# First sum of h in the head, scans issued with their scores, and shifted filler rates in a two-layer decoder trunk

## The chip, the core and the metric

One NeuronCore of a Trainium2 chip runs the whole program. TensorE (PE) multiplies matrices, VectorE (DVE), ScalarE (ACT) and GpSimd (POOL) do elementwise work, SyncE (SP) issues the DMAs. The metric is the device time of one execution in microseconds (us); the time of the kernel before is the median of three runs.

## The reference

Two layers, each on a residual stream x of 1024 tokens by 1024 features, all in float32:

```python
h = rmsnorm(x, norm1[l])
proj = h @ w_in[l]
qa, ka, va, qb, kb, vb, gate_pre = jnp.split(proj, splits, axis=-1)
o_a = dilated_mixture(hd4(qa), hd4(ka), hd4(va))          # 3 groups x 4 heads, softmax with ALiBi
o_b = stick_breaking_attention(hd4(qb), hd4(kb), hd4(vb)) # 4 heads
gates = jax.nn.sigmoid(gate_pre + b_gate[l])
merged = g_a * (o_a @ w_br[l, :OUT_A]) + g_b * (o_b @ w_br[l, OUT_A:])
x = x + merged @ w_o[l]
# then: rmsnorm, up-projection, causal depthwise conv, gelu * value, down-projection, residual
```

In stick-breaking attention a query's weight on a key is sigmoid(z) times the product of (1 - sigmoid(z)) over all later keys up to the query: a product that runs backwards along the row of keys.

## The kernel before

**Arithmetic.** Every float32 factor is kept as two parts, hi (rounded to the matmul's type) and lo (the rest): `split` makes them, hi with a cast on ACT (L141) and lo with a subtraction on DVE (L146). A product is three matmuls of 128 x 512: hi·hi, hi·lo, lo·hi. Larger products (`pair`, `up`, `down`) are done on 2 x 2 blocks with seven block products instead of eight; for these the blocks of h, called b11, b12, b21 and b22 in the code, have to be added and subtracted first, into S[1], S[2], S[3] and S[4], each four tiles of 128 x 512 in two parts. `block_sums` does that: S[3] begins from b22 and b12, S[1] from b12 and b11, each with three POOL operations per tile (L988, L993, L994); S[2] comes from S[1] and b22, S[4] from S[2] and b21, with two DVE operations per tile (L1004, L1005); each is then split in two.

**The mixer of a layer.** Its first part is the head: values, keys and queries of the first two stick heads by plain products (`values_part`, `kq_half`), while the last parts of h are still being made. Then `attend` goes through a list of items: 16 stick items (`stick_item`, four heads by four blocks of 256 queries, the longest block first), four near items (`near_item`, window attention with dilation 1) and 16 far items (`far_item`, the two dilated groups). An item has steps: scores into the PSUM banks "s" (L619, L620); exponentials or sigmoids on ACT; turns (transposes of the weights by PE, then a split in two); applies (products with the values). `attend` issues the next item's scores between the steps of the current one.

In a stick item, a row's scores get the causal mask on DVE (L683), two sigmoids on ACT (L684 into beta, L685 into stay), and then the backward product, a scan on DVE (L697), and a product of beta with it (L701). The scans wait in a list, SCANS; `turn` takes from it what its own transposes need and then two more.

**The filler.** All other projections of the layer are done between these steps, so that PE has work while the other engines make the weights: four gates as plain products (`gate`, 8 shares each), ten pairs of keys, queries and values, and six pairs of gates (`pair`, 14 shares each). A share is six matmuls of 128 x 512. `Dense.advance(rate)` is called once after each step of an item and adds the rate to what is due; whole shares are issued. The rates are RATE for stick items (by the block's length, RATE[3] for the longest), RATE_N for near and RATE_T for far ones. Where a fetch is not there, `until` issues shares until it is declared done, a fixed number of shares after its issue: LEAD for stick rows and far items, LEAD_N for near items. What filler is left behind the last item, `finish` issues, and then come the rest of the two joins of the branches, the split of the branch inputs and the branch products (`br_ps`).

`advance` and `until` also call `aside`, which takes one entry from the list that `block_sums` returned, if the names it needs are done ("plain": the four plain gates).

**What sets the order.** PE's order is the program's, as issued. DVE, ACT and POOL are ordered by the compiler's planner by priorities and its own costs (in the feed-forward part their order is fixed too); some orders are tied by hand with add_manual_dep. All engines then take their work strictly in that order. DMAs go through SP's queue.

**Buffers.** Tiles come from rotating sets by tag: "xa" has four (stick rows' keys and values, their queries, the stay tiles, later the far items' keys and queries), "ql" two (the value tiles of the head, then each pair's weights `in_a`), "e8" six (among them S[1] to S[3], later the parts of the branch inputs), "pt" six small ones. The temporary of the sums, h_sum, is one xa tile that is held from the first sum to the end of S[4].

Of the kernel before, what the change touches and what calls it, by code (L numbers as in the profile page):

```python
# [7 lines left out]
F32 = mybir.dt.float32  # L8
# [4 lines left out]
ALU = mybir.AluOpType  # L13
# [3 lines left out]
P = 128  # L17
# [3 lines left out]
HF = 512  # L21
# [6 lines left out]
SCALE = 0.125  # L28
# [12 lines left out]
IN_ORDER = {ET.PE, ET.Activation, ET.DVE, ET.Pool}  # L41
HEAD = 4
SECOND = 0.35
RATE = (1.0, 1.15, 1.25, 1.3)
RATE_N = 0.85
RATE_T = 0.75
PLAIN = 4
LEAD = 6
LEAD_N = 9
AHEAD_B = 3  # L50
X_AT = (3, 5, 7, 9)
AHEAD = 200
# [3 lines left out]
def f32(ap):  # L56
    return ap.bitcast(F32)
# [3 lines left out]
def trunk_kernel(ctx, tc, x, norm1, w_in, b_gate, w_br, w_o, norm2, w_up, conv_w, conv_b, w_down, norm_f, out, depth=None, probe=None):  # L61
# [156 lines left out]
    class Dense:  # L218
# [38 lines left out]
        def fetch(self):  # L257


            def there(i):  # L260
                return i < 16 and {"N11", f"1{i // 8}", f"2{i // 8}", "v1", "v2"} <= self.done

            def row(j):
                return j < 16 and f"K{j // 4}" in self.done and self.rows >= j - 3

            def row_v(j):
                return j < self.b and self.free[3 - j % 4] >= j // 4

            def whole(v):
                return v < 4 and self.b == 16 and self.rows == 16 and {f"K{4 + v}", f"V{4 + v}"} <= self.done and self.near >= v  # L270

            while row(self.b):
                fetch_row(self.b)
                self.at(LEAD, lambda j=self.b: self.done.add(f"FB{j}"))
                self.b += 1
            while row_v(self.bv):
                fetch_values(self.bv)
                self.bv += 1
            while whole(self.n):
                fetch_whole(self.n)  # L280
                self.at(LEAD_N, lambda v=self.n: self.done.add(f"FN{v}"))
                self.n += 1
            while self.kq < self.scored + 2 and there(self.kq):
                fetch_kq(self.kq)
                self.at(LEAD, lambda i=self.kq: self.done.add(f"F{i}"))
                self.kq += 1
            while self.v < self.applied + 4 and there(self.v):
                fetch_v(self.v)
                self.v += 1
# [217 lines left out]
    def norm(n, gain, tag, then=None, keep=False):  # L507
        acc = ACC[n]
        ss = sb.tile([P, 8], F32, tag="ss", bufs=2, name="ss")
        yield  # L510
        tot = bank(tag, "nrm_t")
        for c in range(4):
            pe.matmul(tot[:, c : c + 1], acc[:, c * P : (c + 1) * P], ones, start=True, stop=True, skip_group_check=True)
        yield
        act.activation(ss[:, 0:4], tot[:, 0:4], AF.Sqrt, bias=eps[:, 0:1], scale=1.0 / D)
        dve.reciprocal(ss[:, 4:8], ss[:, 0:4])
        if then:
            table(then, ss[:, 4:5])
        yield
        rb = bank(tag, "nrm_b")  # L520
        for c in range(4):
            pe.transpose(rb[:, c * P : (c + 1) * P], ss[:, 4 + c : 5 + c].to_broadcast([P, P]), ident)
        yield
        new_h(n)
        for e in range(KD):
            hf = kept_f32(n, e) if keep else small("hf")
            dve.scalar_tensor_tensor(hf, xc(n, e), gain[:, e : e + 1], rb, ALU.mult, ALU.mult)
            hi, lo = H[n][0][:, e, :], H[n][1][:, e, :]
            act.copy(hi, hf)
            (pool if e % 2 and not (keep and n) else dve).tensor_tensor(lo, hf, f32(hi), ALU.subtract)  # L530
            if e < KD - 1:
                yield

# [42 lines left out]
    def in_parts(c, scale, hi, lo, x):  # L576
        if c:
            act.mul(hi, x, scale)
            return dve.scalar_tensor_tensor(lo, x, scale, f32(hi), ALU.mult, ALU.subtract)
        act.copy(hi, x)  # L580
        return dve.tensor_tensor(lo, x, f32(hi), ALU.subtract)

    def kq_half(c, w, n):
        o = bank("ps", "kq_ps"[c:])
        yield from product(o, [(w[k], h_part(n, k)) for k in range(KD)])
        hi, lo = small("kq_h", F32R), small("kq_l", F32R)
        LAST["head"] = in_parts(c, SCALE, hi, lo, o).ins.name
        keep_kq(c, n, 0, hi, lo)
        yield

# [74 lines left out]
    def stick_item(dense, u, qp):  # L665
# [4 lines left out]
        def score(a):  # L670
            L = P * (2 * qp + a + 1)
            bt = rows[a] = sb.tile([P, T], F32, tag="p4", bufs=4, name="beta")
            if a == 0:
                st[0] = sb.tile([P, 2, T], F32, tag="xa", bufs=4, name="stay")
            sv = st[0][:, a, :]
            for c1 in range(L, 0, -512):
                c0 = max(0, c1 - 512)
                w = c1 - c0
                z = bank("s", "z")
                scores(z[:, :w], *(q[:, x, a * P : a * P + P] for x in range(2)), k[:, c0:c1])  # L680
                with tc.high_priority(offset=AHEAD):
                    if c1 == L:
                        dve.tensor_tensor(z[:, w - P : w], z[:, w - P : w], mask_b, ALU.add)  # L683
                    act.activation(bt[:, c0:c1], z[:, :w], AF.Sigmoid)  # L684
                    act.activation(sv[:, c0:c1], z[:, :w], AF.Sigmoid, scale=-1.0)  # L685
                (SCANS if c1 == L else left).append((shared, bt, sv, c0, c1, L))
            if a:
                SCANS.extend(left)
                dense.rows += 1

        def scans(most):

# [284 lines left out]
    def block_sums(more):  # L977


        keep = {}  # L980

        def first(t, a, b, i):
            if i == 0:
                if "r" not in keep:
                    keep["r"] = quarter("h_sum")
                new_s(t)
            r, (ah, al), (bh, bl) = keep["r"][:, i, :], a()[i], b()[i]
            one = pool.tensor_tensor(r, f32(al), f32(bl), ALU.subtract)  # L988
            if "last" in keep:
                tc.add_manual_dep(one.ins, keep["last"], NO_SYNC, reason="one sum after the other")  # L990
            else:
                tc.add_manual_dep(one.ins, LAST["head"], SYNC, reason="after the first projections")
            pool.tensor_tensor(r, r, f32(ah), ALU.add)  # L993
            keep["last"] = pool.tensor_tensor(r, r, f32(bh), ALU.subtract).ins.name  # L994

        def further(t, a, i):
            if t == 4:

                S[4] = half(0, 0)
            less(a, i)  # L1000

        def less(a, i):
            r, (ah, al) = keep["r"][:, i, :], a()[i]
            dve.tensor_tensor(r, f32(ah), r, ALU.subtract)  # L1004
            dve.tensor_tensor(r, r, f32(al), ALU.add)  # L1005

        def in_two(t, i):
            split(*S[t][i], keep["r"][:, i, :], "waits")

        b11, b12, b21, b22 = (lambda n=n, k=k: half(n, k) for k in range(2) for n in (1, 0))  # L1010
        todo = []

        def series(after, t, f, lag, gap):

            at = {}
            for i in range(4):
                at.setdefault(i * gap, []).append(lambda i=i: f(i))
                at.setdefault(i * gap + lag, []).append(lambda i=i: in_two(t, i))
            for k in range(3 * gap + lag + 1):
                todo.append((after, lambda fs=at.get(k, ()): [g() for g in fs]))  # L1020

        series(set(), 3, lambda i: first(3, b22, b12, i), 3, 2)
        series(set(), 1, lambda i: first(1, b12, b11, i), 3, 2)
        for i in range(4):
            todo.append((set(), lambda i=i: less(b22, i)))
        series(set(), 2, lambda i: i or new_s(2), 0, 1)
        todo += more
        series({"plain"}, 4, lambda i: further(4, b21, i), 1, 1)
        return todo

    def zeros():
# [179 lines left out]
    def mixer(l, pending):  # L1211
# [7 lines left out]
        if l:  # L1219
# [3 lines left out]
                for _ in range(HEAD if i == 0 else i % 3 > 0):  # L1223
                    next(units, None)
            for _ in units:
                pass
        else:
            first_units = relay(head(l))

# [10 lines left out]
                if i == 1:  # L1240
                    next(vectors)
            for _ in first_units:
                pass
        for _ in vectors:
            pass
        dense.main = [
# [624 lines left out]
    def first():  # L1871
# [64 lines left out]
        def normed(i):  # L1936

            n, c = i // 4, i % 4
            if c == 0:
                new_h(n)  # L1940
            rb = bank("o", "x_rb")
            pe.transpose(rb[:, 0:P], factor[i][:, 2:3].to_broadcast([P, P]), ident)
            for h in range(2):
                hf = small("hf").rearrange("p (e t) -> p e t", e=4)
                for k in range(4 * h, 4 * h + 4):
                    dve.scalar_tensor_tensor(hf[:, k - 4 * h, :], part[i][:, k, :], g0[:, k : k + 1], rb[:, 0:P], ALU.mult, ALU.mult)
                split(*(y[:, 4 * h : 4 * h + 4, c * P : (c + 1) * P] for y in H[n]), hf)

        def in_two(i, *halves):
            n, c = i // 4, i % 4  # L1950
# [116 lines left out]
```

## Time and profile before

| | |
|---|---|
| median of 3 runs | 2725.03 us (2724.64 to 2726.55) |
| the profiled execution | 2720.71 us, of which the span is 2718.9 us |
| granted TensorE clock, mean | 0.992 |
| PE busy | 2648.2 us |
| DVE busy | 2079.8 us |
| ACT busy | 1341.5 us |
| POOL busy | 680.1 us |

Times in the profile are microseconds from the start of the span. A row of instructions gives start, duration, engine, line of the kernel, operation, output and inputs; in brackets stands how long the engine had been idle before it and what released it. A row of a wait gives who waited for whom, the total, the number of times and the longest. A row of a group gives busy time, mean ns of one, and the idle time before. Matmuls are pipelined: in an undisturbed stretch the starts tell their rate, not the durations.

### The profile page before, as it was taken

The page shows a single profiled execution, that of the slowest core. Times are in us where ns is not written, and L with a number is a line of the kernel's source. Part 1 is how long each engine was busy: PE and PEld are TensorE (multiplying, and loading weights), DVE is VectorE, ACT ScalarE, POOL GpSimd, SP SyncE. Part 2 cuts the span into 40 slices and gives each one's busy share as a digit, 9 for nine tenths or more (in the row PEclk, how much of TensorE's full clock was granted, in tenths as well). Part 3 has the DMA queues.
Part 4 walks back from the last instruction along what each step waited for, and adds up shares of the span by engine and source line. Part 5 has one row for each costly group of instructions (what it writes and reads, how often), then busy time and mean ns, then how long its engine had stood idle before and what let it go on. Part 6 is the DMA issues. An engine that isn't in the chain of part 4 may idle for free. (4 is left out here: it accounts for less than half of the span.)

```text
span 2718.9 us, 36768 instructions
## 1 busy us (share of the span) xinstructions
PE 2648.2 (97%) x12780; PEld 2204.5 (81%) x12780; DVE 2079.8 (76%) x3151; ACT 1341.5 (49%) x2488; POOL 680.1 (25%) x483
## 2 busy tenths in 40 slices
PE   9899999989999999999999999999899999999999
PEld 8677788878888888888887778888788888888888
DVE  5787766676789888897649777656858888998865
ACT  5455555555455545432335555654745545554225
POOL 2601011013124433421152011010312433443210
PEclk9999999989999999999999999999899999999999
DMA  8456576564334444588452657755732444546863
GB/s 276 117 136 168 150 205 194 191 229 151 93 117 158 145 155 140 212 326 312 177 159 78 162 154 191 207 171 181 268 97 82 148 150 145 171 140 250 330 250 122
DMA packets 418918, 482.95 MB, mean 178 GB/s; under 512 B 26420, under 2 KB 336044, under 8 KB 416940
## 3 DMA queue, kind: packets, MB, share of 16 engines
q1 hardware_dynamic: 418716, 480.59, 55.1%
q8 instruction: 101, 1.65, 0.3%
q14 instruction: 85, 0.70, 0.1%
q10 hardware_dynamic: 16, 0.00, 0.0%
HBM read 307.43 MB, written 173.08 MB: 177 GB/s over the span
## 5 line engine op out<-in xcount | busy, mean ns | idle before, releaser
L146 DVE TENSOR_TENSOR w_lo<-up_a,w_hi 128x512 fp32r<-128x512 f32 x240 | 237.8, 997 | 20.6 <-ACT w_hi L141 20.6
L141 ACT CAST w_hi<-up_a 128x512 fp32r<-128x512 f32 x240 | 149.4, 622 | 184.3 <-PE u_a L972 45.1
L1062 POOL TENSOR_TENSOR u<-in_a 128x512 f32<-128x512 f32 x32 | 44.1, 1380 | 702.1 <-DMA in_a<-in_w_in_dram 165.8
L1703 DVE TENSOR_TENSOR x<-x,d_ps 128x512 f32<-128x512 f32 (+1 forms) x228 | 151.8, 671 | 77.9 <-PE d_ps L1697 76.5
L1434 POOL TENSOR_TENSOR cv<-cv 128x512 f32<-128x512 f32 x88 | 132.3, 1516 | 250.0 <-DVE cv L1429 133.5
L141 ACT CAST w_hi<-in_a 128x512 fp32r<-128x512 f32 x192 | 119.5, 623 | 129.7 <-PE i_c L972 39.7
L146 DVE TENSOR_TENSOR w_lo<-in_a,w_hi 128x512 fp32r<-128x512 f32 x192 | 138.3, 722 | 56.6 <-ACT w_hi L141 52.3
L146 DVE TENSOR_TENSOR g<-cv,g 128x512 fp32r<-128x512 f32 x154 | 152.0, 988 | 5.2 <-ACT g L141 2.7
L1695 PE MATMUL d_ps<-gd_in,w_hi 128*128 128x512 f32 (+1 forms) x340 | 130.4, 384 | 1.6 <-issue 0.8
L1697 PE MATMUL d_ps<-gd_in,w_lo 128*128 128x512 f32 (+1 forms) x340 | 129.8, 382 | 0.0
L1696 PE MATMUL d_ps<-gd_in,w_hi 128*128 128x512 f32 (+1 forms) x340 | 129.8, 382 | 0.0
L971 PE MATMUL u_a<-hh,w_hi 128*128 128x512 f32 x320 | 124.7, 390 | 0.8 <-DVE u L1585 0.8
L973 PE MATMUL u_a<-hh,w_lo 128*128 128x512 f32 x320 | 124.5, 389 | 0.0
L972 PE MATMUL u_a<-t_lo,w_hi 128*128 128x512 f32 x320 | 124.5, 389 | 0.0
L971 PE MATMUL u_a<-t_hi,w_hi 128*128 128x512 f32 x320 | 124.5, 389 | 0.0
L972 PE MATMUL u_a<-hl,w_hi 128*128 128x512 f32 x320 | 124.5, 389 | 0.0
L973 PE MATMUL u_a<-t_hi,w_lo 128*128 128x512 f32 x320 | 124.5, 389 | 0.0
L146 DVE TENSOR_TENSOR w_lo<-w_raw,w_hi 128x512 fp32r<-128x512 f32 x96 | 75.6, 791 | 56.4 <-ACT w_hi L141 55.3
L141 ACT CAST g<-cv 128x512 fp32r<-128x512 f32 x154 | 94.9, 616 | 40.4 <-POOL cv L1434 29.8
L1695 PE MATMUL d_ps<-gd_in,wd 128*128 128x512 f32 (+1 forms) x292 | 113.9, 390 | 0.0
L1697 PE MATMUL d_ps<-gd_in,wd 128*128 128x512 f32 (+1 forms) x292 | 112.8, 386 | 0.0
L1696 PE MATMUL d_ps<-gd_in,wd 128*128 128x512 f32 (+1 forms) x292 | 112.8, 386 | 0.0
(394 smaller groups left out, 8556.0 us busy)
## 6 DMA issues: line engine op xcount, KB each, us to landing
gd<-g SPq DMA_DIRECT2D x154, 512.0 KB, 3.5
gd_in<-gd SPq DMA_DIRECT2D x154, 512.0 KB, 6.1
up_a<-in_w_up_dram SPq DMA_DIRECT2D x80, 512.0 KB, 5.7
in_a<-in_w_in_dram SPq DMA_DIRECT2D x64, 512.0 KB, 5.2
t_kq<-tk SPq DMA_DIRECT2D x32, 768.0 KB, 4.5
wd_raw<-in_w_down_dram SPq DMA_DIRECT2D x22, 1024.0 KB, 12.0
gin<-gs SPq DMA_DIRECT2D x32, 512.0 KB, 4.3
w_raw<-in_w_o_dram SPq DMA_DIRECT2D x64, 256.0 KB, 2.9
```

Source lines behind the costliest of these rows:

```text
L141: one = act.copy(hi, src)
L146: two = dve.tensor_tensor(lo, src, f32(hi), ALU.subtract)
L971: pe.matmul(o, w[0][:, c], rh, start=(first and i == 0), stop=False, skip_group_check=True)
L972: pe.matmul(o, w[0][:, c], rl, start=False, stop=False, skip_group_check=True)
L973: pe.matmul(o, w[1][:, c], rh, start=False, stop=(last and i == 3), skip_group_check=True)
L1062: pool.tensor_tensor(u2, a11, a21, ALU.subtract)
L1434: return lambda: pool.tensor_tensor(dst, a, b, ALU.subtract)
L1695: pe.matmul(o[:, sub], wh[:, c], gh[:, sub], start=(i == 0 and k in (0, 4, 5)), stop=False, skip_group_check=True)
L1696: pe.matmul(o[:, sub], wh[:, c], gl[:, sub], start=False, stop=False, skip_group_check=True)
L1697: pe.matmul(o[:, sub], wl[:, c], gh[:, sub], start=False, stop=(i == m - 1), skip_group_check=True)
L1703: dve.tensor_tensor(x, x, o[:, sub], ALU.add)
```

## The change

- S[3] is begun in the head: the entries of the sums are also taken there, one per step of the head that is left when all of h is made; the first POOL operation waits for the last part of h (LAST["h"]) instead of for the first projections (LAST["head"]). S[1] and what follows need the new name "head", which is set when the head has been issued.
- The temporaries: S[3] has an xa tile of its own, given back when S[3] is made; S[1] and S[2] share a tile of the tag ql; S[4] is made from S[2]'s two parts with three DVE operations per tile in small tiles.
- A stick item issues two entries of SCANS right behind its second row of scores.
- The rates: stick items 1.0, 1.15, 1.25, 1.3 become 1.15, 1.3, 1.4, 1.45; near items 0.85 becomes 0.75; far items 0.75 becomes 0.5. LEAD_N goes from 9 to 7, and far items' fetches are declared done after LEAD_T = 3 shares instead of 6.

```diff
-RATE = (1.0, 1.15, 1.25, 1.3)
-RATE_N = 0.85
-RATE_T = 0.75
+RATE = (1.15, 1.3, 1.4, 1.45)
+RATE_N = 0.75
+RATE_T = 0.5
...
-LEAD_N = 9
+LEAD_N = 7
+LEAD_T = 3
...
-                self.at(LEAD, lambda i=self.kq: self.done.add(f"F{i}"))
+                self.at(LEAD_T, lambda i=self.kq: self.done.add(f"F{i}"))
...
             if a:
                 SCANS.extend(left)
                 dense.rows += 1
+                scans(2)
...
-            r, (ah, al), (bh, bl) = keep["r"][:, i, :], a()[i], b()[i]
+            rs[t] = quarter("h_sum") if t == 3 else sb.tile([P, 4, HF], F32, tag="ql", bufs=2, name="h_sum")
+            r, (ah, al), (bh, bl) = rs[t][:, i, :], a()[i], b()[i]
             one = pool.tensor_tensor(r, f32(al), f32(bl), ALU.subtract)
...
-                tc.add_manual_dep(one.ins, LAST["head"], SYNC, reason="after the first projections")
+                tc.add_manual_dep(one.ins, LAST["h"], SYNC, reason="after h")
...
+        def second(i):
+            if i == 0:
+                new_s(2)
+            in_two(1, i)
+            r, (ah, al) = rs[1][:, i, :], b22()[i]
             dve.tensor_tensor(r, f32(ah), r, ALU.subtract)
             dve.tensor_tensor(r, r, f32(al), ALU.add)
+        def fourth(i):
+            if i == 0:
+                S[4] = half(0, 0)
+            r, (ah, al) = small("h_sum"), b21()[i]
+            dve.tensor_tensor(r, f32(ah), f32(S[2][i][0]), ALU.subtract)
+            dve.tensor_tensor(r, r, f32(S[2][i][1]), ALU.subtract)
+            dve.tensor_tensor(r, r, f32(al), ALU.add)
+            split(*S[4][i], r, "waits")
...
-        series(set(), 3, lambda i: first(3, b22, b12, i), 3, 2)
-        series(set(), 1, lambda i: first(1, b12, b11, i), 3, 2)
-        for i in range(4):
-            todo.append((set(), lambda i=i: less(b22, i)))
-        series(set(), 2, lambda i: i or new_s(2), 0, 1)
+        series(set(), 3, 2, lambda i: first(3, b22, b12, i), lambda i: in_two(3, i))
+        series({"head"}, 3, 2, lambda i: first(1, b12, b11, i), second)
+        for i in range(4):
+            todo.append((set(), lambda i=i: in_two(2, i)))
         todo += more
-        series({"plain"}, 4, lambda i: further(4, b21, i), 1, 1)
+        for i in range(4):
+            todo.append(({"plain"}, lambda i=i: fourth(i)))
...
             for _ in first_units:
-                pass
+                dense.aside()
+        dense.done.add("head")
```

More of the change, by code (lines that the diff above doesn't have):

```diff
@@ L529, in norm @@
             act.copy(hi, hf)
-            (pool if e % 2 and not (keep and n) else dve).tensor_tensor(lo, hf, f32(hi), ALU.subtract)
+            LAST["h"] = (pool if e % 2 and not (keep and n) else dve).tensor_tensor(lo, hf, f32(hi), ALU.subtract).ins.name
             if e < KD - 1:
@@ L578, in in_parts @@
             act.mul(hi, x, scale)
-            return dve.scalar_tensor_tensor(lo, x, scale, f32(hi), ALU.mult, ALU.subtract)
-        act.copy(hi, x)
-        return dve.tensor_tensor(lo, x, f32(hi), ALU.subtract)
+            dve.scalar_tensor_tensor(lo, x, scale, f32(hi), ALU.mult, ALU.subtract)
+        else:
+            act.copy(hi, x)
+            dve.tensor_tensor(lo, x, f32(hi), ALU.subtract)
     def kq_half(c, w, n):
@@ L586, in kq_half @@
         hi, lo = small("kq_h", F32R), small("kq_l", F32R)
-        LAST["head"] = in_parts(c, SCALE, hi, lo, o).ins.name
+        in_parts(c, SCALE, hi, lo, o)
         keep_kq(c, n, 0, hi, lo)
@@ L977, in block_sums @@
     def block_sums(more):
-        keep = {}
+        last, rs = {}, {}
         def first(t, a, b, i):
             if i == 0:
-                if "r" not in keep:
-                    keep["r"] = quarter("h_sum")
                 new_s(t)
-            r, (ah, al), (bh, bl) = keep["r"][:, i, :], a()[i], b()[i]
+                rs[t] = quarter("h_sum") if t == 3 else sb.tile([P, 4, HF], F32, tag="ql", bufs=2, name="h_sum")
+            r, (ah, al), (bh, bl) = rs[t][:, i, :], a()[i], b()[i]
             one = pool.tensor_tensor(r, f32(al), f32(bl), ALU.subtract)
-            if "last" in keep:
-                tc.add_manual_dep(one.ins, keep["last"], NO_SYNC, reason="one sum after the other")
+            if last:
+                tc.add_manual_dep(one.ins, last["sum"], NO_SYNC, reason="one sum after the other")
@@ L991, in first @@
             else:
-                tc.add_manual_dep(one.ins, LAST["head"], SYNC, reason="after the first projections")
+                tc.add_manual_dep(one.ins, LAST["h"], SYNC, reason="after h")
             pool.tensor_tensor(r, r, f32(ah), ALU.add)
[L994 to L1003, printed above, removed]
+            last["sum"] = pool.tensor_tensor(r, r, f32(bh), ALU.subtract).ins.name
@@ L1007, in in_two, with series @@
         def in_two(t, i):
-            split(*S[t][i], keep["r"][:, i, :], "waits")
+            split(*S[t][i], rs[3 if t == 3 else 1][:, i, :], "waits")
         b11, b12, b21, b22 = (lambda n=n, k=k: half(n, k) for k in range(2) for n in (1, 0))
         todo = []
-        def series(after, t, f, lag, gap):
+        def series(after, lag, gap, f, g):
             at = {}
@@ L1017, in series @@
                 at.setdefault(i * gap, []).append(lambda i=i: f(i))
-                at.setdefault(i * gap + lag, []).append(lambda i=i: in_two(t, i))
+                at.setdefault(i * gap + lag, []).append(lambda i=i: g(i))
             for k in range(3 * gap + lag + 1):
-                todo.append((after, lambda fs=at.get(k, ()): [g() for g in fs]))
-        series(set(), 3, lambda i: first(3, b22, b12, i), 3, 2)
-        series(set(), 1, lambda i: first(1, b12, b11, i), 3, 2)
+                todo.append((after, lambda fs=at.get(k, ()): [h() for h in fs]))
+        series(set(), 3, 2, lambda i: first(3, b22, b12, i), lambda i: in_two(3, i))
+        series({"head"}, 3, 2, lambda i: first(1, b12, b11, i), second)
         for i in range(4):
-            todo.append((set(), lambda i=i: less(b22, i)))
-        series(set(), 2, lambda i: i or new_s(2), 0, 1)
+            todo.append((set(), lambda i=i: in_two(2, i)))
         todo += more
-        series({"plain"}, 4, lambda i: further(4, b21, i), 1, 1)
+        for i in range(4):
+            todo.append(({"plain"}, lambda i=i: fourth(i)))
         return todo
@@ L1242, in mixer @@
             for _ in first_units:
-                pass
+                dense.aside()
+        dense.done.add("head")
         for _ in vectors:
@@ L1946, in normed @@
                     dve.scalar_tensor_tensor(hf[:, k - 4 * h, :], part[i][:, k, :], g0[:, k : k + 1], rb[:, 0:P], ALU.mult, ALU.mult)
-                split(*(y[:, 4 * h : 4 * h + 4, c * P : (c + 1) * P] for y in H[n]), hf)
+                LAST["h"] = split(*(y[:, 4 * h : 4 * h + 4, c * P : (c + 1) * P] for y in H[n]), hf).ins.name
         def in_two(i, *halves):
```

## The prediction

> **What bounds the kernel.** I read the page first, then the windows by stage, then who waited for whom, then the order of single instructions where the waits are. The page gives TensorE as the bound:
>
> ```profile
> span 2718.9 us, 36768 instructions
> PE 2648.2 (97%) x12780; PEld 2204.5 (81%) x12780; DVE 2079.8 (76%) x3151; ACT 1341.5 (49%) x2488; POOL 680.1 (25%) x483
> t_kq<-tk SPq DMA_DIRECT2D x32, 768.0 KB, 4.5
> ```
>
> No matmul is added or removed, so only time in which PE stands or runs at a low granted clock can be won: 70.7 us, and some clock. The windows say where it lies. Columns: window, its length, busy of PE, PEld, DVE, ACT, POOL (us), granted clock, DMA share, GB/s. In layer 0 the opening of the stick items is 64:130, their rest 130:358, the near items 358:470, the far items 470:564, the end of the mixer 564:602; in layer 1 the opening is 1413:1470, the rest 1470:1698, the end 1904:1942.
>
> ```profile
> 64.00:130.00 66.00, 54.72 (x250) 44.08 (x249) 49.51 (x62) 26.19 (x51) 44.21 (x29) 0.92 0.46 130
> 130.00:358.00 228.00, 217.46 (x1101) 178.39 (x1100) 179.77 (x301) 124.91 (x254) 23.16 (x16) 1.00 0.59 156
> 358.00:470.00 112.00, 110.91 (x582) 93.61 (x581) 70.83 (x161) 62.89 (x151) 11.03 (x8) 1.00 0.66 190
> 470.00:564.00 94.00, 92.09 (x538) 79.37 (x537) 60.49 (x135) 47.56 (x112) 9.09 (x8) 1.00 0.56 183
> 564.00:602.00 38.00, 29.01 (x149) 23.65 (x148) 29.13 (x58) 23.74 (x49) 5.39 (x5) 0.82 0.74 266
> 602.00:1390.00 788.00, 785.89 (x3526) 650.84 (x3525) 641.57 (x826) 367.17 (x592) 247.91 (x168) 1.00 0.52 179
> 1413.00:1470.00 57.00, 53.38 (x257) 43.22 (x257) 45.16 (x62) 25.00 (x51) 32.72 (x21) 1.00 0.37 112
> 1470.00:1698.00 228.00, 217.88 (x1098) 179.01 (x1097) 180.25 (x301) 123.73 (x252) 22.70 (x16) 0.99 0.59 157
> 1904.00:1942.00 38.00, 30.90 (x156) 25.91 (x156) 29.77 (x60) 24.89 (x51) 5.79 (x5) 0.82 0.74 266
> ```
>
> PE stands 11.3 us in the opening of layer 0, 10.5 in its stick items, 9.0 at its end; 3.6, 10.1 and 7.1 in layer 1. The 788 us between the mixers lose 2.1 and are left aside.
>
> **The opening.** Who made PE wait in 64:130, and the instructions behind the longest wait, on POOL, ACT, DVE and PE:
>
> ```profile
> PE z L619 <- ACT stay L685: 10.1, 2, 7.0
> PE sb_t L709 <- DVE beta L701: 1.2, 1, 1.2
> ```
>
> ```profile
> 66.17 1.30 POOL L988 TENSOR_TENSOR h_sum<-hl 128x512 f32<-128x512 f32 x1
> 104.62 1.61 POOL L994 TENSOR_TENSOR h_sum<-h_sum,hh 128x512 f32<-128x512 f32 x1
> 78.86 0.62 ACT L141 CAST t_hi<-h_sum 128x512 fp32r<-128x512 f32 x1 [3.20 <-POOL h_sum L994]
> 80.53 3.41 DVE L146 TENSOR_TENSOR w_lo<-w_raw,w_hi 128x512 fp32r<-128x512 f32 x2
> 83.87 0.28 DVE L683 TENSOR_TENSOR z<-z,mask_b 128x128 f32<-128x128 f32 x1
> 100.50 0.77 ACT L685 ACTIVATE stay<-z 128x512 f32<-128x512 f32 x2 [3.20 <-DVE beta L701]
> 41.91 0.69 DVE L146 TENSOR_TENSOR hl<-hf,hh 128x512 fp32r<-128x512 f32 x1 [0.69 <-ACT hh L141]
> 85.32 0.80 PE L619 MATMUL z<-kv,slots 128*128 128x512 f32 x1 [7.00 <-ACT stay L685]
> 87.62 0.63 PE L179 MATMUL g_ps<-hl,w_hi 128*128 128x512 f32 x1
> 88.05 0.63 PE L180 MATMUL g_ps<-hh,w_lo 128*128 128x512 f32 x1
> ```
>
> The 24 POOL operations of the two sums run from 66.2 to 106.2, over the first scores. ACT takes its work in order and stands 3.2 us for a sum at 78.86; DVE's w_lo take 1.7 us each, and the mask waits for them. The 3.1 us wait at 101 is the second of the two: ACT stood for the stay tile, of which xa had one free while h_sum held another. h itself was done at 42.6 (41.91 + 0.69).
>
> **1. Sums of h.** Emitted in the head, the twelve POOL operations of S3 can follow h from 42.6; at 1.3 us they end near 59, and those of S1, emitted behind the head, near 77, about where the first scores come. The head has room:
>
> ```profile
> 40.00:60.00 20.00, 20.00 (x135) 18.53 (x134) 6.43 (x12) 5.08 (x9) 0.00 (x0) 1.00 0.88 259
> 1402.94 1.29 POOL L988 TENSOR_TENSOR h_sum<-hl 128x512 f32<-128x512 f32 x1 [14.72 <-DVE kq_l L579]
> ```
>
> It takes four ACT casts and four DVE subtractions there (about 0.6 and 0.7 us each), costed at nothing. ACT's queue then holds the head's evacuations behind a cast that waits for three POOL operations, 3.9 us; two PSUM banks of 5.4 us (24 matmuls) cover that, and were they not to, the price is a few times 1 us. S1's sum takes a ql slot, which leaves one for weights until S2 is made, before the second pair loads; S3's xa slot is back before the second stay tile is wanted. fourth() has three DVE operations where further() had two: 4 x 2 x 0.7 = 5.6 us of DVE, hidden while DVE is 79% busy (179.77 of 228). POOL's memsets of none and slots, about 1 us each, wait on neither sum; SP gets no DMA more. In layer 1 the sum waited 14.7 us for the head's last projection, the same room.
>
> Layer 0: 11.3 us of standing fall to 2.0. The ends are 0 and layer 1's 3.6, which still has POOL's sums in it; I take the middle. Won 9.3. The clock: matmuls 0.43 apart (87.62, 88.05) instead of 0.23 (below) from 85.3 to 88.5; 0.92 over 66 us is 5.3 us of clock, of which some 3.0 met work. Together 12.3. Layer 1: 3.6 to 2.0, won 1.6.
>
> **2. Scans with the scores.** In the rest of the stick items of layer 0 and layer 1 the wait that answers to late scans, and DVE's rows of 130:358:
>
> ```profile
> PE sb_t L709 <- DVE beta L701: 2.9, 4, 1.1
> PE sb_t L709 <- DVE beta L701: 2.8, 4, 1.1
> L697 DVE TENSOR_TENSOR_SCAN stay<-stay,zero 128x512 f32<-128x512 f32 x19 | 24.9, 1310 | 2.7 <-ACT stay L685 2.7
> L701 DVE TENSOR_TENSOR beta<-beta,stay 128x512 f32<-128x512 f32 x12 | 8.1, 678 | 0.0
> 1480.00:1500.00 20.00, 17.02 (x73) 13.12 (x72) 16.88 (x31) 11.85 (x24) 0.00 (x0) 0.91 0.27 66
> ```
>
> Nothing is added; two scans and two products per item (up to 2 x 1.31 + 2 x 0.68 = 4.0 us) go ahead of whatever DVE gets next: the filler's w_lo and the next item's mask. They can win 5.7 at most and, by delays of other waits, lose; I take 4.0. The low clock after the waits of 1483 to 1487 (0.91 of 20 us, 1.5 us of work) goes with them. Together 5.5, between 7.2 and a loss of 19 (a rival).
>
> The Trainium skill, "TensorE: Matmul & The Clock Gate", section "What's actually happening", says that the clock halves after at least one idle window of about 3.4 us. The 7.0 us wait agrees; at 1480 no wait for sb_t was over 1.1 us and yet the clock fell. By that rule this step would not hang on these waits, the 1.5 us would stay, and the sum would be 33.3.
>
> **3. The filler.** A share is six matmuls of filler; its length and the last share of layer 0:
>
> ```profile
> 562.34 0.40 PE L971 MATMUL i_a<-hh,w_hi 128*128 128x512 f32 x1
> 562.57 0.40 PE L972 MATMUL i_a<-hl,w_hi 128*128 128x512 f32 x1
> 563.50 0.39 PE L973 MATMUL i_a<-hh,w_lo 128*128 128x512 f32 x1
> 563.73 0.28 PE L888 MATMUL o<-p1h,slots 128*128 128x256 f32 x1
> PE o L888 <- ACT p1h L141: 5.2, 4, 1.9
> PE o L888 <- DVE p1l L146: 0.8, 4, 0.2
> PE j_ps L942 <- POOL fx L928: 1.1, 2, 0.9
> PE br_ps L179 <- DVE ol_a L146: 1.8, 1, 1.8
> 367.17 1.27 SPq L1126 DMA_DIRECT2D tk<-in_a x2
> ```
>
> 563.73 - 562.34 = 1.39 us a share. Four gates of 8 and sixteen units of 14 make 256. Stick items ask 10, 8, 6, 4 times at the four rates: 33.9 shares for four items before, 38.1 after. With what attend() forces while a fetch is awaited I count 141 in stick items before and 153 after, 64 and 51 in near items, and 43 in far items, all used up behind the scores of the thirteenth of sixteen, which is where the trace has the last one. After, far items take 40, through the last, and four stand behind it, ahead of and between the two joins. So some 12 shares, 16.7 us of PE work, move into the end of each mixer, from near items (PE 110.91 of 112) that need less cover.
>
> The end loses 9.0 us standing and 0.18 x 29.0 = 5.2 of clock in layer 0, 7.1 and 0.18 x 30.9 = 5.6 in layer 1. What stays: the factors and the split of on (1.1 + 1.8, that is 2.9) and one low-clock step as at 85 (3.2 us at half speed, 1.6); in layer 1 4.0 instead of 4.5. Won 9.7 and 8.7, 18.4; bounds 0 and 22. The buffers of the branch inputs come free only with the last gate, ten shares later than now, hence not all of it.
>
> Stick items take 12 shares more at 1.39 us, near items fewer: moved, not added. With them one pair's 20 stores pass on SP from the near into the stick items, 20 x 0.64 = 12.7 us of issue in the 20 us and more of a unit; costed at nothing, and where a fetch stood behind them, at about 1 us. Near at 0 (bounds -3 and 0). Far items have 2.5 shares where they had 3.3: 2.5 x 1.39 = 3.5 us besides some 2.4 of their own, against DVE's work of 60.49/13 = 4.7 us an item now, 4.2 then; PE still ends last, but with less slack: I take -1.5 a layer, -3. F is declared three shares after its fetch: 4.2 us and the pieces between, against 4.5 to landing; the fetch is issued two items ahead, some 11 us. LEAD_N 7 shares is 9.7 us. Both at nothing; if they were short, about 1 us for each of four near and one or two far starts.
>
> **The sum** against the profiled execution's 2720.71 (span 2718.9): 12.3 + 1.6 + 5.5 + 18.4 - 3 = 34.8, so 2685.9. That execution stands 4.3 under the median of 2725.03; with the median, 2690.2.
>
> **The rivals.**
> *The far items starve (slower).* Place: all 32 far items. Without filler PE waited 5.2 + 0.8 us in the five and a half items behind 563.7: 1.1 us an item, at clock 0.82. If 2.5 shares don't cover the chain from scores to exp to split, 32 x 1.1 = 35 us go, which cancels the gain: from 1.1 us an item it is slower. With half the clock loss of that stretch (0.09 of 32 x 5.9 = 17 us) it is 2690 + 52 = 2742. For it: DVE 4.2 of 5.9 us. Against: 92.09 of 94 at 3.3 shares.
> *The scans delay masks and splits.* If each of 32 items costs PE 0.6 us for a burst of 4.0 on a DVE that is 79% busy, 19 us, and the 5.5 fall away: 2714. Against: the mask is issued with priority, so one scan at most stands before it.
> *The first sum doesn't come earlier*, because the order of POOL or a buffer holds it: the change doesn't do what it says, the opening's 13.9 fall away, 2704. Against: POOL 0.00 in 40:60.
> *More goes than I count*: with more filler also the other half of the stick items' 20.6 us, or all of the end: some 14 us more, 2676.
>
> **Chances.** Forecast 0.55 (alone 2678 to 2702), starving 0.11, scans 0.14, sum 0.08, more 0.12. A measurement tells 0.2%, 5.5 us, from nothing. Faster: 0.55 + 0.08 + 0.12 + three quarters of the scans' case, 0.85; within 0.2% 0.04; slower 0.11. The range 2666 to 2720 holds all but the starving and some of the edges.
>
> **What would show it.** The first h_sum near 43 and 1389 on POOL and the last before the second scores; no wait over 2 us on z; sb_t waiting under 1 us in each stick stage; filler matmuls up to the joins; clock 1.00 in the openings and above 0.9 at the ends. It would be wrong if p1h or z held PE through the far items, if masks stood behind scans, or if the end kept its standing with filler in it, because the branch inputs come that much later.

## The result, and the profile after

The changed kernel took 2702.26 us (median of four runs, 2693.10 to 2702.97), the kernel before on the same chip 2724.84. The ratio is 0.9911 with a 95% interval of 0.9888 to 0.9934: 0.9% faster, where the prediction had 2690 us. Every kernel below computes the whole reference; they differ in orders, buffers and rates alone. Three executions of the kernels below took far longer than the others (2907.80, 3501.09 and 9349.45 us) and are left out of all medians and ratios here.

The profiled execution after (2701.9 us), first lines of the page:

```profile
span 2700.0 us, 36777 instructions
PE 2635.3 (98%) x12780; PEld 2201.9 (82%) x12780; DVE 2084.5 (77%) x3159; ACT 1342.1 (50%) x2488; POOL 673.6 (25%) x483
```

Windows of the same execution, in the columns of the prediction's windows (bounds, length, busy of PE, PEld, DVE, ACT, POOL, granted clock, DMA share, GB/s). The stages are shifted by up to 20 us against those of before; the stretches 0:64 and 60:72 are added.

```profile
0.00:64.00 64.00, 57.22 (x382) 51.83 (x382) 37.20 (x89) 35.97 (x71) 34.30 (x41) 0.98 0.72 225
60.00:72.00 12.00, 0.05 (x1) 0.05 (x1) 7.89 (x7) 3.38 (x6) 11.61 (x9) 0.58 0.15 43
64.00:130.00 66.00, 54.02 (x239) 43.48 (x240) 44.19 (x60) 26.82 (x51) 19.03 (x13) 0.89 0.60 172
130.00:358.00 228.00, 218.05 (x1102) 180.63 (x1102) 183.01 (x296) 122.17 (x244) 26.98 (x18) 1.00 0.56 147
564.00:602.00 38.00, 37.38 (x192) 31.23 (x191) 33.10 (x59) 24.23 (x46) 8.26 (x8) 1.00 0.79 284
1385.00:1413.00 28.00, 20.93 (x131) 19.13 (x129) 11.18 (x11) 5.47 (x11) 26.90 (x21) 0.88 0.45 113
1904.00:1942.00 38.00, 38.00 (x183) 31.81 (x182) 34.77 (x46) 24.50 (x40) 10.43 (x9) 1.00 0.86 311
```

The ends, which lost 9.0 and 7.1 us of standing at a clock of 0.82, are nearly full: 37.38 of 38 and 38.00 of 38, both at 1.00. (Layer 1's end now comes some 15 us earlier; from 1889 to 1927 PE is busy 37.33 us, also at 1.00.) But PE does next to nothing from 60 to 72, in the head, where it had been full. Who made it wait in 64:130 and, below, in 1385:1413:

```profile
PE q_ps L179 <- DVE vb L558: 12.0, 1, 12.0
PE g_ps L179 <- DVE kq_l L583: 2.2, 1, 2.2
PE z L621 <- ACT stay L687: 1.8, 2, 1.6
...
PE v_ps L179 <- DVE kq_l L583: 7.1, 1, 7.1
```

The 7.0 us wait of the first scores for the stay tile is down to 1.6. In its place each head has a wait that was not there: for the evacuation of a PSUM bank (PE's products go into these banks, and a bank can be used again when ACT and DVE have read its product out, as for vb, kq_h and kq_l). The order of the instructions on POOL, ACT, DVE and PE in the two heads:

```profile
42.30 1.30 POOL L990 TENSOR_TENSOR h_sum<-hl 128x512 f32<-128x512 f32 x1 [13.88 <-DVE hl L147]
52.23 0.58 ACT L557 CAST vb<-v_ps 128x512 fp32r<-128x512 f32 x1
56.01 0.62 ACT L142 CAST t_hi<-h_sum 128x512 fp32r<-128x512 f32 x1 [3.19 <-POOL h_sum L996]
60.32 0.62 ACT L142 CAST t_hi<-h_sum 128x512 fp32r<-128x512 f32 x1 [3.68 <-POOL h_sum L996]
64.55 0.62 ACT L142 CAST t_hi<-h_sum 128x512 fp32r<-128x512 f32 x1 [3.61 <-POOL h_sum L996]
69.11 0.62 ACT L142 CAST t_hi<-h_sum 128x512 fp32r<-128x512 f32 x1 [2.90 <-POOL h_sum L996]
69.64 0.58 ACT L557 CAST vb<-v_ps 128x512 fp32r<-128x512 f32 x1
71.22 0.68 DVE L558 TENSOR_TENSOR vb<-v_ps,vb 128x512 fp32r<-128x512 f32 x1
71.95 0.79 PE L179 MATMUL q_ps<-hh,kq_w 128*128 128x512 f32 x1 [12.04 <-DVE vb L558]
74.14 0.62 ACT L142 CAST t_hi<-h_sum 128x512 fp32r<-128x512 f32 x1 [3.92 <-POOL h_sum L996]
75.70 0.58 ACT L582 CAST kq_h<-kq_ps 128x512 fp32r<-128x512 f32 x1
81.47 0.68 DVE L583 TENSOR_TENSOR kq_l<-kq_ps,kq_h 128x512 fp32r<-128x512 f32 x1
82.20 0.69 PE L179 MATMUL g_ps<-hh,w_hi 128*128 128x512 f32 x1 [2.21 <-DVE kq_l L583]
...
1379.15 1.28 POOL L990 TENSOR_TENSOR h_sum<-hl 128x512 f32<-128x512 f32 x1
1397.07 0.62 ACT L142 CAST t_hi<-h_sum 128x512 fp32r<-128x512 f32 x1 [3.61 <-POOL h_sum L996]
1397.59 0.58 ACT L582 CAST kq_h<-kq_ps 128x512 fp32r<-128x512 f32 x1
1399.45 0.58 PE L179 MATMUL v_ps<-v_w,hh 128*128 128x256 f32 x1 [7.07 <-DVE kq_l L583]
```

Read it along ACT. The first four casts into t_hi, of which those of 56.01 and 60.32 are shown, are S[3]'s; the next ones, from 64.55, are S[1]'s. Between vb's two casts (52.23 and 69.64) lie 17.4 us in which ACT takes four casts of sums, each waiting about 3 to 4 us for POOL to finish three more operations. The bank that vb frees is the one the q projection needs, so PE stands 12.0 us behind POOL's pace. It stands 2.2 once more for the next evacuation: kq_h is cast at 75.70, but DVE comes to kq_l only at 81.47, behind operations that are slow beside POOL (last section). In layer 1 the cast of S[3]'s last tile stands ahead of kq_h in the same way: 7.1 us.

To put the whole on one scale, I took the starts of consecutive PE instructions and summed by how much they lie farther apart than the median for the same tile and shape in the kernel before (smaller distances count against larger ones). That counts standing and low clock together. Stages are bounded by the first kq_ps, score, near, far and o_ps matmuls of each layer; us, both layers added:

| stage | before | after | sums alone | rates and scans | rates alone | scans alone | all, sums behind the head | all, splits behind the head |
|---|---|---|---|---|---|---|---|---|
| head and plain gates | 0.7 | 28.3 | 27.4 | 0.7 | 0.7 | 0.7 | 0.7 | 0.4 |
| stick items | 51.2 | 33.1 | 35.7 | 44.0 | 49.1 | 52.5 | 62.1 | 36.8 |
| near items | 2.7 | 1.0 | 2.6 | 0.4 | 0.4 | 2.7 | 0.4 | 1.3 |
| far items to the end of the mixer | 31.6 | 5.7 | 27.9 | 4.1 | 3.3 | 30.7 | 4.2 | 4.7 |
| sum | 86.1 | 68.2 | 93.6 | 49.1 | 53.5 | 86.6 | 67.4 | 43.3 |

The sums differ as the spans do (after 17.9 against 18.9 us of span; rates alone 32.6 against 32.8). So the change won 18.1 us in the stick items, 1.7 in the near ones and 25.8 from the far items on, 45.5 together, and paid 27.6 of it back in the heads.

### The profile page after: what moved, and what is told of

The parts are those of the page before. It is cut to its first block, busy times and chain, and to the rows that moved or that the text cites. A ratio compares the mean times of both kernels' runs of the same rounds, so it can differ in the third digit from the quotient of the medians.

```text
span 2700.0 us, 36777 instructions
## 1 busy us (share of the span) xinstructions
PE 2635.3 (98%) x12780; PEld 2201.9 (82%) x12780; DVE 2084.5 (77%) x3159; ACT 1342.1 (50%) x2488; POOL 673.6 (25%) x483
## 4 chain that ended last, share of the span: by engine, by line
PE 81%; DVE 9%; ACT 2%; DMA 2%; issue 2%; POOL 1%; SPq 0%; DVEq 0%; ACTq 0%; POOLq 0%
PE u_a L974 5%; PE u_a L975 5%; PE u_a L976 5%; PE d_ps L1704 4%; PE d_ps L1705 4%; PE d_ps L1706 4%; PE i_a L974 3%; PE i_a L976 3%; PE i_a L975 3%; PE u_c L974 3%; PE u_c L976 3%; PE u_c L975 3%; PE o_ps L179 2%; PE o_ps L181 2%; PE o_ps L180 2%; PE i_c L974 2%
```

## The experiments

All are timed against the kernel before on the same chip: 2718.56 us for the first four of them, 2721.51 for the next four, 2721.54 for the last. The theory formed from the two traces: the heads pay for the order of ACT and DVE behind POOL's sums, and the filler rates bring most of the gain. Its rivals: POOL's traffic itself slows the head; the scans bring the gain.

**The sums alone.** The kernel before with `block_sums` and the head of the change, the rates and `scans(2)` left out (shown in part, against the changed kernel):

```diff
-RATE = (1.15, 1.3, 1.4, 1.45)
+RATE = (1.0, 1.15, 1.25, 1.3)
...
-                scans(2)
```

> The kernel before with the sums of the change alone (head, buffers, S[4]); rates, leads and scans as before. Theory: the heads lose 26 us, the openings win 10 to 14, so slower than before: 2738. By the prediction's term (openings win 13.9, the head costs nothing): 2711.

Measured 2728.34 us, ratio 1.0033 (1.0022 to 1.0045): alone this part makes the kernel slower. Who waited in its first 130 us and, below, in 1380:1470:

```profile
PE q_ps L178 <- DVE vb L557: 12.0, 1, 12.0
PE z L620 <- ACT stay L686: 1.8, 2, 1.6
...
PE v_ps L178 <- DVE kq_l L582: 7.1, 1, 7.1
```

Both forecasts count from 2725; from this chip's 2718.56 they come to about 2732 and 2705, and the measurement is near the theory's. The waits are those of after. Its stick items lose 15.5 us less than before's (51.2 to 35.7), and its heads 26.8 more. The prediction's terms for this part, 12.3 + 1.6 = 13.9, and the cost nothing stand against these two numbers.

**Without the sums.** The rates and scans on the kernel before:

> The kernel before with the scans and the rates of the change, but with its own sums of h (start, xa tile, S[4] from the running sum). Theory: the ends gain as after the change, the opening of layer 0 keeps its 7.0 us wait: 2702 - 26 + 16 = 2692, faster than the change. If the sums in the head were what made the change faster, 2715 or more.

Measured 2686.8 us, ratio 0.9873 (0.9857 to 0.9890): faster than the whole change. The 7.0 us wait for the stay tile remains, and yet leaving out the sums is a gain.

**All sums behind the head.** The change, but S[3] begins, like S[1], when the head has been issued, with the new buffers and the new `fourth`:

```diff
-        series(set(), 3, 2, lambda i: first(3, b22, b12, i), lambda i: in_two(3, i))
+        series({"head"}, 3, 2, lambda i: first(3, b22, b12, i), lambda i: in_two(3, i))
...
-                tc.add_manual_dep(one.ins, LAST["h"], SYNC, reason="after h")
+                tc.add_manual_dep(one.ins, LAST["head"], SYNC, reason="after the first projections")
```

> All of the change, but the first sum starts behind the first projections, as before the change; its temporaries stay in the idle buffers. Theory: the heads are as before (36 and 34 us), the openings lose about what they lost before, less the 3.1 us wait for the stay tile: 2702 - 26 + 8 = 2684. If the head's stall had been paid back in the opening, 2702 or more.

Measured 2700.87 us, ratio 0.9933 (0.9916 to 0.9950), 14 us slower than leaving the sums as they were: a miss for my theory too. The head is undisturbed, but the new buffers do not help the opening, and a new wait comes in. In 64:175 of this run:

```profile
PE z L620 <- ACT stay L686: 10.9, 2, 7.0
PE i_c L973 <- ACT u L1090: 5.2, 1, 5.2
```

The wait for the stay tile is as long as before (7.0): as long as S[3] begins late, the new buffers don't cure it (its temporary holds an xa tile then as well). The 5.2 us fall at the start of the first pair, where all of S[4] is issued. ACT's copy into u runs at 147.96, behind two casts of S[4] that had waited 2.14 us for DVE's sums. Whether S[4]'s third DVE operation or only the place of these casts makes the wait was not separated.

**POOL's sums in the head, their splits behind it.** The change, with the twelve POOL operations of S[3] issued as there, but the four casts and subtractions only when the head has been issued, and tied behind its last evacuations on ACT (`split` with "waits" already puts its cast behind LAST["act"]; kq_h sets it in the same way as vb, shown below):

```diff
-        series(set(), 3, 2, lambda i: first(3, b22, b12, i), lambda i: in_two(3, i))
+        for i in range(4):
+            todo.append((set(), lambda i=i: first(3, b22, b12, i)))
+        for i in range(4):
+            todo.append(({"head"}, lambda i=i: in_two(3, i)))
...
+            LAST["act"] = act.copy(vv[:, :, :, 0:64], ov).ins.name
```

> POOL's first sum stays in the head; its four splits (ACT cast, DVE subtraction) are issued behind the head and ordered after the head's last evacuation on ACT. Theory (the head stalls because ACT and DVE hold the evacuations of PSUM behind casts that wait for POOL): the 12.0 and 7.1 us waits in the heads go, kq_ps to the first gate falls from 53.4 and 43.1 us back to about 36 and 34, the openings stay as short as after the change, 2702 - 26 + 2 = 2678. Rival (POOL beside DVE, not the order, slows the head): half of the 26 us stays, 2690. Second rival (the work has to be done somewhere, and the opening pays for it): near 2700.

Measured 2676.31 us, ratio 0.9844 (0.9828 to 0.9861): faster than both kernels, and 10.5 us faster than the rates and scans with the sums left where they were, on the same chip. The window 0:64 of this run, and ACT's order in its head:

```profile
0.00:64.00 64.00, 61.94 (x404) 56.10 (x405) 38.99 (x91) 37.02 (x73) 33.23 (x41) 1.00 0.84 262
...
53.75 0.59 ACT L557 CAST vb<-v_ps 128x512 fp32r<-128x512 f32 x1 [0.82 <-PE v_ps L181]
59.26 0.59 ACT L582 CAST kq_h<-kq_ps 128x512 fp32r<-128x512 f32 x1
64.66 0.60 ACT L579 ACTIVATE kq_h<-q_ps 128x512 fp32r<-128x512 f32 x1 [4.81 <-PE q_ps L181]
65.15 2.69 ACT L142 CAST t_hi<-h_sum 128x512 fp32r<-128x512 f32 x5
```

POOL is as busy in the head as after (33.23 against 34.30 us), and PE is not held: vb and kq_h go as soon as PE is done with them, and five waiting casts (S[3]'s four and one of S[1]) go behind them in one piece. The order caused the stall, not POOL's traffic.

**The rates alone, the scans alone.** Each put into the kernel before.

> The kernel before with the new filler rates and leads alone; sums of h and scans as they were. By the prediction's terms (ends 18.4, near 0, far -3) it is 15.4 us faster than the kernel before, which took 2718.6 on this chip: about 2703. By the theory formed since, the run with rates and scans together (2686.9) owes nearly all of its 31.7 us to the rates: between 2685 and 2690, with the stretch from the first gate to the end of the mixer some 18 us shorter in each layer.

Measured 2693.94 us, ratio 0.9902 (0.9879 to 0.9924), between what the theory and the prediction's terms gave. The loss from the far items on falls from 31.6 to 3.3. Its profiled execution (2688.06 us) is the fastest of the four; by the medians the rates win 27.6 us, not the table's 32.6.

> The kernel before with the scans issued behind the scores alone; rates and sums as they were. By the prediction's term 5.5 us faster, 2713. By the rival (scans and products stand ahead of other DVE work) the waits of sb_t for DVE go, but waits of v_t and sb_o for DVE come in their place, and the time is that of the kernel before within 0.2%, 2713.5 to 2724.

Measured 2719.37 us, ratio 0.9994 (0.9984 to 1.0003): no gain. Its waits in 130:358:

```profile
PE i_a L972 <- DVE u L1098: 1.9, 1, 1.9
PE v_t L1154 <- DVE vv L1159: 1.8, 2, 1.3
PE sb_t L710 <- DVE beta L702: 0.6, 1, 0.6
```

The transposes wait 0.6 us for beta instead of 2.9, as the change means them to, but filler stands for u and for the transposed values, which now come later on DVE.

**Old stick rates, new near and far rates**, on the kernel before, without scans or sums (shown against the rates alone):

```diff
-RATE = (1.15, 1.3, 1.4, 1.45)
+RATE = (1.0, 1.15, 1.25, 1.3)
```

> The kernel before with the new rates of the near and the far items and the new leads, but the old rates of the stick items; no new sums, no new scans. If only the filler kept for the end counts, as the prediction has it, it equals the run with all rates (within 4 us of it), the stick items as long as before and the end covered. If the stick items gain from their 12 further shares too, it is 6 to 14 us slower than that run, with the 10 us that PE stands in the stick items of each layer unchanged.

Measured 2692.86 us, ratio 0.9901 (0.9880 to 0.9921): equal to all rates together. In this run the 53 us up to the output product are full:

```profile
570.00:623.00 53.00, 53.00 (x236) 43.88 (x235) 46.02 (x65) 34.00 (x58) 19.41 (x14) 1.00 0.74 238
```

**Scans and stick rates, as a square.** First the kernel with the splits behind the head without its scans, then the four corners on one chip: stick rates new or old, `scans(2)` or not, in the kernel with the splits behind the head.

> The run with POOL's sum in the head and its splits behind it (2676.3), less the scans issued behind the scores. If the scans are worth the prediction's 5.5 us, about 2682; if they trade one wait for another, 2673 to 2679, with waits of sb_t for DVE back at 1 us each and those of v_t for u gone.

Measured 2686.18 us, ratio 0.9871 (0.9851 to 0.9892): slower than both forecasts, but on another chip than the kernel that it is set against.

> The run with POOL's sum in the head and its splits behind it, again, as one corner of a square: stick rates new or old, scans behind the scores or not, all on one chip. Theory: the scans are worth something only with the new stick rates, since in the old ones a later transpose or filler product waited for DVE instead. Then this corner is the fastest, 0.984 to 0.986 of the kernel before. Rival: the scans are worth as much with either rates in this kernel, whose opening stands less.

> Second corner: new stick rates, no scans behind the scores. By theory and rival alike 7 to 12 us slower than the first corner (it was 12.4 us of span on another chip): 0.987 to 0.989 of the kernel before.

> Third corner: old stick rates, scans behind the scores; near and far rates new. By the theory no faster than the fourth corner by more than 3 us, and 5 to 10 us slower than the first. By the rival 7 to 12 us faster than the fourth, and equal to the first within 3 us, since without the scans the stick rates made no difference (2693.9 and 2694.1).

> Fourth corner: old stick rates, no scans behind the scores; near and far rates new. Both: as the second corner within 4 us, 0.986 to 0.989 of the kernel before, since the stick rates alone made no difference.

| | with scans | without |
|---|---|---|
| new stick rates | 2680.76 us, 0.9850 (0.9836 to 0.9865) | 2684.33 us, 0.9875 (0.9857 to 0.9892) |
| old stick rates | 2687.56 us, 0.9874 (0.9859 to 0.9889) | 2683.38 us, 0.9862 (0.9847 to 0.9876) |

By the medians the scans win 3.6 us with the new stick rates, where 7 to 12 were expected, and lose 4.2 with the old ones. That is the sign of the theory, but the intervals of the corners overlap, so neither side is settled by itself. With the new rates three comparisons agree in sign (this one; rates with scans against rates alone, 0.9873 and 0.9902; the best kernel and the same without scans, 0.9844 and 0.9871), each by about 0.25 to 0.3% of the ratios (by the medians of this square only 0.13%), the last two across chips. Waits in 130:358 of the first, second and third corner:

```profile
PE v_t L1165 <- DVE u L1104: 2.6, 1, 2.6
PE i_c L975 <- ACT gt L1210: 2.0, 1, 2.0
...
PE sb_t L712 <- DVE beta L704: 3.7, 3, 2.8
PE v_t L1164 <- DVE vv L1169: 2.9, 2, 2.7
...
PE z L622 <- issue: 3.4, 1, 3.4
PE i_c L975 <- ACT gt L1210: 3.2, 1, 3.2
PE i_a L975 <- DVE u L1109: 1.9, 1, 1.9
```

Each corner has its own two or three waits of 2 to 3 us; a few tenths of a per cent depend on which of DVE's products comes first, and I can name no rule for it. The best kernel repeats: 0.9844 on one chip, 0.9850 on this one.

## Why the prediction was right and wrong

The time lay in the range of 2666 to 2720 and the sign was right, but 2702.26 is just outside the 2678 to 2702 that stood for the forecast alone, and that it came so near is partly luck. Two errors of opposite sign met: 27.6 us were lost in the heads, and elsewhere 10.7 more were won than forecast (45.5 against 34.8). With the first error alone 7.2 us of gain would have been left.

*The head, costed at nothing: the step that failed.* It read "ACT's queue then holds the head's evacuations behind a cast that waits for three POOL operations, 3.9 us; two PSUM banks of 5.4 us (24 matmuls) cover that, and were they not to, the price is a few times 1 us". It counted one cast ahead of an evacuation. The trace has four in a row between vb's two casts, two of them of S[1], which is issued behind the head. The stall is then POOL's pace times the number of casts, 17.4 us from vb to vb, and two banks cover 5.4. DVE stands behind the same casts. Measured 27.6 us in the two heads after, 26.8 for the sums alone, and nothing when the casts are tied behind the evacuations. The bound that I should have taken is the length of POOL's series less the banks.

*The opening.* 12.3 + 1.6 for the two layers; the sums alone won 15.5 in the stick items. The mechanism (sums over the first scores) is borne out, since the wait for z keeps its 7.0 us where only the start of the sums is put back. In layer 0 the first 77 us of stick items lost 16.8 before and 6.6 with the sums alone, 10.2 for the 12.3. Layer 1 was undersized: there they lost 11.2 and 5.0, against 1.6 forecast from standing alone, without the clock. About half of this lies in the opening itself, up to 1470, where waits of 1.3, 1.7 and 0.4 us shrank to one of 0.5; the rest lies behind it, in waits and a low clock that the sum had booked under the scans. POOL's first h_sum came at 42.30 and 1379.15, where 43 and 1389 were forecast; layer 1's head itself begins 9 us earlier than before.

*Scans, 5.5.* With the old rates they win nothing, with the new ones about 4 to 8 us (rates with scans less rates alone, 0.9902 - 0.9873 of 2720). So the size fits the change as a whole, within intervals that overlap, but not for the reason given: the rival of the scans that delay other DVE work is real, at the size of the gain. After, the 2.9 us of waits for beta are gone and these stand in 130:358 and 1470:1698:

```profile
PE v_t L1161 <- DVE u L1100: 2.6, 1, 2.6
PE sb_o L725 <- DVE sbl L147: 1.7, 1, 1.7
...
PE sb_o L725 <- DVE sbl L147: 2.2, 1, 2.2
```

*The clock at 1480.* The second of those waits is also a test of the rule cited from the Trainium skill, "TensorE: Matmul & The Clock Gate", section "What's actually happening". The wait, the granted clock just behind it, and the clock where it had been 0.91:

```profile
1471.70 0.58 PE L725 MATMUL sb_o<-sbl,kv 128*128 128x256 f32 x1 [2.19 <-DVE sbl L147]
...
1472.00:1474.00 2.00, 2.00 (x7) 1.71 (x7) 2.00 (x5) 0.00 (x0) 0.00 (x0) 0.50 0.00 0
1480.00:1490.00 10.00, 10.00 (x54) 8.34 (x53) 7.06 (x14) 4.95 (x11) 0.00 (x0) 1.00 0.38 93
```

Where the waits for sb_t went, the clock is back at 1.00, and it was 0.50 behind a wait of 2.19 us eight us earlier. The rule's idle window of about 3.4 us is longer than that wait, so here the measurement decides. The low clock went with the short waits, as the sum had it, but it came again with the next wait (0.83 from 1470 to 1480) and was not won. Nor is it the scans alone that take the short waits away: with the sums alone, and the old scans, the same stretch of the stage (1493 to 1513) has two waits of 0.6 and 0.8 us and a clock of 1.00.

*The ends, 18.4, and the far items, -3.* Together 15.4; measured 25.8 after and 28.3 with the rates alone. The step is the right one: the old stick rates give the same time, so what counts is filler kept back by the near and far items, with their leads. Two sizes were off. The standing that I left (2.9 and one step of the clock, 4.5 and 4.0 in all) is covered too: from the first br_ps to the first o_ps nothing is lost. And the far items did not pay for their thinner filler: 2.5 shares an item are enough, and the starving rival did not occur. Near items, at 0, won 1.7.

*The other rivals.* The first sum did come earlier; that this rival's 2704 lies near the measured time is chance. "More goes than I count" is true of the ends, where 10.4 us more went than forecast. Of what would show the theory right, the waits for z (1.6 at most), the filler up to the joins and the clock of the ends (1.00) are there. The window 64:130 of layer 0 shows a clock of 0.89 because the stall in the head falls into it now; from 94, where the first scores are, the clock is 1.00, so this sign is there too.

Terms against measurement: 13.9 + 5.5 became 18.1 in the stick items, 18.4 - 3 became 25.8, near 0 became 1.7, and the head's 0 became -27.6. Forecast 34.8, measured 17.9 by the table.

## What to carry to other kernels

When work for a slow engine is moved into a full stretch, look at which in-order queue its consumers join, and bound the price by the whole series of the slow engine's operations over the cover in PSUM banks, not by one wait. Emit the slow operations early and the operations that wait for them late: with the new rates and scans, POOL's sums in the head with their splits behind it won 1.5%, the same sums with their splits in between 0.9%, and the sums left where they were 1.3%; the sums in the head alone, with their splits in between, lost 0.3%. Filler is worth most where the chain between engines is longest, here at the joins; taking it from stages that PE fills anyway cost nothing here.

## What the runs showed of the hardware

How long a DVE operation of 128 x 512 takes depends here on what it reads and on POOL. DVE in the head after, while POOL adds without a break until 79.2, and then once it has stopped:

```profile
60.97 1.09 DVE L147 TENSOR_TENSOR t_lo<-h_sum,t_hi 128x512 fp32r<-128x512 f32 x1 [3.19 <-ACT t_hi L142]
76.27 3.47 DVE L147 TENSOR_TENSOR w_lo<-w_raw,w_hi 128x512 fp32r<-128x512 f32 x2
80.87 0.68 DVE L1004 TENSOR_TENSOR h_sum<-h_sum,hl 128x512 f32<-128x512 f32 x1
```

With two operands in SBUF an operation takes 1.1 to 1.7 us beside POOL and 0.68 without it. The subtraction of vb at 71.22, with one operand in PSUM, takes 0.68 beside POOL. While POOL adds, DVE's operations on SBUF there thus take 1.6 to 2.5 times as long, and in the kernel with the splits behind the head PE pays nothing for it in the head. The cause of the difference is not shown by these rows.
